# A two-layer decoder trunk on one core: the first layer's GpSimd steps named for VectorE, a third PSUM bank for its output projection, sixteen turning transfers recorded over other pairs

## The chip, the cores and the metric

One core of one Trainium2 chip. The time is the device time of one execution in microseconds (us); the median of three runs is compared. TensorE (PE in the profile) multiplies, ScalarE (ACT), VectorE (DVE) and GpSimd (POOL) do the elementwise work, SyncE (SP) only issues DMAs. GpSimd issues some DMAs too.

## The reference

Input x is 1024 tokens by 1024 features, float32. Layer 0 is gated linear attention with 4 heads (key width 128, value width 256), layer 1 is dilated sliding-window attention with 8 query heads in 3 groups over one shared K/V. Cut to the part that the change touches:

```python
# layer 0
q, k, v, g, a_lr = split(x @ w_in)
log_a = log_sigmoid(a_lr @ w_a2 + b_a2) / 16          # per head and key channel
b = cumsum(log_a)                                      # within a chunk
o_t = q_t S_t,  S_t = diag(exp(log_a_t)) S_{t-1} + k_t^T v_t
o = o * rsqrt(mean(o * o) + 1e-5) * norm_g
x1 = layer_norm(alpha * x + (o * silu(g)) @ w_out)
# layer 1
k_sh, v_sh = rope(x1 @ w_k), x1 @ w_v
out = layer_norm(alpha * x1 + (windowed_attention(rope(x1 @ w_q), k_sh, v_sh) * silu(x1 @ w_g)) @ w_out2)
```

## The kernel before, in words

Matrices are kept in a float32 form that TensorE multiplies in three passes: each operand is split in a high part (`split_hi`, always on ACT) and a low part (`split_lo`, the difference, recorded as `S.vp`), and a product is high*high, high*low, low*high. That holds for weights (`wf` loaded, `wh` and `wl` split from it) and for activations.

The program is recorded step by step with an object `S` and then ordered by a planner (`Sched.order`). The planner gives every step a cost, keeps a clock for each engine, and again and again takes the step that can start first; among steps that could start at the same time it takes the one recorded earlier (`prio`, which `S.later(n)` moves by n). A step recorded as `S.vector` goes to DVE, one recorded as `S.vp` to DVE or POOL, whichever the planner can start first (if DVE could start as early and is cheaper, DVE). The planner lets no two steps of DVE and POOL that read SBUF in the same way overlap (`shares_port`). The result is a fixed order of instructions for each engine; on the chip each engine runs its own list in that order and waits on semaphores. All instructions are issued from one line of the planner (L469), so the profile's groups are told apart by tile names, not by lines.

The stages, in order of time:

1. A first projection gives the values of head 0 and the gate's low-rank rows (tiles `pro`), while x is split in `xh` and `xl`.
2. From quarters of x, four sums (`xg`, line 1077 on) feed seven-product block multiplications (`pairs`, tiles `sev`), which give q and k of all heads; between them `gate(h)` computes b per head (tiles `sp`, `mn`), and `ahead(3)` computes the seven level factors of head 3 (tiles `Xa`) ahead of time.
3. Per head: `levels(h)` makes for each of seven levels L the factor X = exp of differences of b, times q and k (`steps`, four elementwise steps of 128x512 and one exponential), multiplies blocks of X (tiles `lv`) and merges them in `AT`. `state_prep(h)` makes `qe` and `ke`. `chunks(h, g)` runs four chunks of 128 tokens: products with `AT` and with the state `S` into the two banks `po`, then the next state `S` (DVE, from bank `ms`); afterwards it squares, sums (`sq`), and scales the result, and `finish` multiplies by the gate and, for head 3, splits the result in `ogh` and `ogl`. Projections of the values and gates (`vac`, `acc`) are recorded between these and fill TensorE.
4. `out_ln(0, ...)`, once for each half of the tokens: the output projection in eight column blocks `et`, each a group of 24 matmuls in one PSUM bank, then the layer norm. `bank(layer, et)` names the bank; there are two of each of `acc`, `lv`, `po` and `ms`.
5. Layer 1: V, then K and a part of Q in 14 pairs of seven-product multiplications with `rope` after each; in the same stage `turn_x` turns x1 for the last step, in 16 pieces, each a chain of transfers through one buffer (`swx`): a transposing DMA into `xa`, a store `x1p`, a load `xb`, an ACT copy `xc`, a store `x1t`. Then scores and attention per head, and the last projection, which reads `x1t`.

The names that the change touches: `gate` (the step `mn - sp`), `steps` (two of its four elementwise steps, called for 21 levels by `levels` and for 7 by `ahead`), the four `xg` differences per quarter, `state_prep` (two steps of `ke`), `chunks` (the sum of the two squares), `bank`, and the loop over the pairs at the end of stage 5.

Of the kernel before, what the change touches and what calls it, by code (L numbers as in the profile page):

```python
# [7 lines left out]
F32 = mybir.dt.float32  # L8
# [617 lines left out]
def trunk(tc, xT, xp, wP, wA, wA12, wAv3, w2, wO, wK, wV0, wV12, wB, wOB, par_d,  # L626
          ident_d, lmask_d, cos_d, sin_d, bmask_d, rmask_d, tri_d, lnr_d, out):
    S = Sched(tc, lat=LAT, pad=PAD)
# [5 lines left out]
    ps = S.pool("ps", space="PSUM")  # L634
# [20 lines left out]
    def hs(half):  # L655
        return slice(half * 512, half * 512 + 512)
# [80 lines left out]
    def blk(x, j):  # L737
        return x[:, j * 128:j * 128 + 128]
# [145 lines left out]
    def layer_a(t2, t1, after):  # L884
# [6 lines left out]
        def front(name, kind, dt=F32):  # L891
            return t0.tile([128, 512], dt, name=name, tag=kind, bufs={"a": NA0, "d": 4}[kind])

        def whole(dt, name):
            return t0.tile([128, T], dt, name=name, tag="X", bufs=4)
# [15 lines left out]
        def keep(name, k, t):  # L911
            hi, lo = quarter(name, k)
            split_hi(hi, t)
            split_lo(lo, t, hi)
# [104 lines left out]
        def gate(h):  # L1019
            b = whole(F32, "b")  # L1020
            made["b", h] = dram.tile([128, T], F32, name=f"mb{h}")
            for half in range(2):
                r = hs(half)
                z = ps.tile([128, 512], F32, name="z", tag="ms", bufs=2)
                S.tensor.matmul(z, w2t[:, h * 128:h * 128 + 128], aT[:, r], start=True, stop=True)
                sp = front("sp", "a")
                S.scalar.activation(sp, z, AF.Abs, bias=b2c[:, h:h + 1])
                S.scalar.activation(sp, sp, AF.Exp, scale=-1.0)
                S.scalar.activation(sp, sp, AF.Ln, bias=onec)
                mn = front("mn", "a")  # L1030
                S.vector.tensor_scalar(mn, z, b2c[:, h:h + 1], 0.0, op0=OP.add, op1=OP.min)
                S.vp.tensor_sub(mn, mn, sp)
                for c0 in (0, 256):
                    S.vector.tensor_tensor_scan(b[:, half * 512 + c0:half * 512 + c0 + 256], smask,
                                                 mn[:, c0:c0 + 256], 0.0, op0=OP.mult, op1=OP.add)
            S.sync.dma_start(made["b", h], b)

        def steps(b, q, k, L, X):
            n = T // (2 * L)
            view = lambda t: t.rearrange("p (n s l) -> p n s l", s=2, l=L)  # L1040
            bv, Xv = view(b), view(X)
            ref = bv[:, :, 0, L - 1:L].to_broadcast([128, n, L])
            S.vector.tensor_sub(Xv[:, :, 1, :], bv[:, :, 1, :], ref)
            S.vp.tensor_sub(Xv[:, :, 0, :], ref, bv[:, :, 0, :])
            S.scalar.activation(X, X, AF.Exp, scale=1.0 / 16.0)
            S.vector.tensor_mul(Xv[:, :, 1, :], Xv[:, :, 1, :], view(q)[:, :, 1, :])
            S.vp.tensor_mul(Xv[:, :, 0, :], Xv[:, :, 0, :], view(k)[:, :, 0, :])

        def ahead(h):
            q, k = spare(F32, "qa"), spare(F32, "ka")  # L1050
# [18 lines left out]
        with S.later(-500):  # L1069
            for k in range(4):  # L1070
                two = []
                for ct in (k, k + 4):
                    x = whole(F32, "xg")
                    S.sync.dma_start(x, xT[ct * 128:ct * 128 + 128])
                    two.append((x[:, hs(0)], x[:, hs(1)]))
                (old, t), (old2, low) = two
                S.vp.tensor_sub(old, t, old)
                S.vp.tensor_sub(t, low, t)
                keep("T3", k, t)
                keep("T1", k, old)  # L1080
                S.vp.tensor_sub(low, low, old)
                S.vp.tensor_sub(old2, old2, low)
                keep("T4", k, old2)
                keep("T2", k, low)

# [156 lines left out]
        def state_prep(h):  # L1242
            q, k, b = H[h]["q"], H[h]["k"], H[h]["b"]
            bc = b.rearrange("p (n c) -> p n c", c=128)
            qe = t2.tile([128, T], F32, name="qe", bufs=1)
            S.scalar.activation(qe, b, AF.Exp, scale=1.0 / 16.0)
            dec = t2.tile([128, NCH], F32, name="dec", bufs=2)
            S.vector.tensor_copy(dec, qe.rearrange("p (n c) -> p n c", c=128)[:, :, 127])
            S.vector.tensor_mul(qe, qe, q)
            ke = xtile(F32, "ke")  # L1250
            S.vp.tensor_sub(ke.rearrange("p (n c) -> p n c", c=128),
                                 bc[:, :, 127:128].to_broadcast([128, NCH, 128]), bc)
            S.scalar.activation(ke, ke, AF.Exp, scale=1.0 / 16.0)
            S.vp.tensor_mul(ke, ke, k)
            kh = t2.tile([128, T], F32, name="kh", bufs=2)
            for g in range(2):
                turn_blocks(kh[:, g * 512:g * 512 + 512],
                            [blk(ke, c) for c in range(4 * g, 4 * g + 4)])
            H[h].update(qe=qe, dec=dec, kh=kh, S=None)

        def chunks(h, g):
            v, qe, dec, kh = (H[h][n] for n in ("v", "qe", "dec", "kh"))
            AT = ATs[h % 2]
            oT = t2.tile([128, 2, 512], F32, name="oT", bufs=2)
            H[h]["oT", g] = oT
            St = H[h]["S"]
            po = [ps.tile([128, 512], F32, name="lv" if h == GH - 1 and g else "po", bufs=2) for _ in range(2)]
            for c in range(4):
                cc = 4 * g + c
                cs = slice(c * 128, c * 128 + 128)  # L1270
                for e in range(2):
                    es = slice(e * 128, e * 128 + 128)
                    out = po[e][:, cs].rearrange("p (s x r) -> p x s r", s=2, x=16)
                    S.tensor.matmul(out, v[g][:, c, es], natural(AT[:, cc, :]), start=True, stop=(cc == 0))
                    if cc:
                        S.tensor.matmul(out, St[:, es], natural(blk(qe, cc)), start=False, stop=True)
                if cc < NCH - 1:
                    pS = ps.tile([128, 256], F32, name="ms", bufs=2)
                    S.tensor.matmul(pS, blk(kh, cc), v[g][:, c, :], start=True, stop=True)
                    Sn = t2.tile([128, 256], F32, name="S", bufs=2)  # L1280
                    with S.later(-EVAC):
                        if cc:
                            S.vector.scalar_tensor_tensor(Sn, St, dec[:, cc:cc + 1], pS, op0=OP.mult, op1=OP.add)
                        else:
                            S.vector.tensor_copy(Sn, pS)
                    St = Sn
            H[h]["S"] = St
            sq = [t2.tile([128, 512], F32, name="sq", bufs=3) for _ in range(2)]
            for e in range(2):
                S.scalar.activation(sq[e], po[e], AF.Square)  # L1290
                S.va.copy(oT[:, e, :], po[e])
            S.vp.tensor_add(sq[0], sq[0], sq[1])
            sh, sl = (t2.tile([128, 512], FR, name="sq", bufs=3) for _ in range(2))
            split_hi(sh, sq[0])
            split_lo(sl, sq[0], sh)
            ss = ps.tile([128, 512], F32, name="ms", bufs=2)
            with S.group():
                S.tensor.matmul(ss, onesr, sh, start=True, stop=False)
                S.tensor.matmul(ss, onesr, sl, start=False, stop=True)
            R = t2.tile([128, 512], F32, name="sq", bufs=3)  # L1300
            rsqrt_rows(R, ss, 1.0 / 256.0, sq[0], epsq)
            for e in range(2):
                S.vector.tensor_mul(oT[:, e, :], oT[:, e, :], R)
# [44 lines left out]
            split_lo(lo[:, hs(half)], f, hi[:, hs(half)])  # L1348

    def bank(layer, et):  # L1350
        return ps.tile([128, 512], F32, name=("acc", "lv", "po")[et % 3 if layer else 0], bufs=2)

    def out_ln(layer, r, w_of, res, emit):
        n = r.stop - r.start
# [124 lines left out]
    def layer_b(xs, early):  # L1479
# [102 lines left out]
        for n, (a, b, g) in enumerate(jobs):  # L1582
            now = w
            if n + 1 < len(jobs):
                w = load_pair([x[0] for x in jobs[n + 1][:2]])
            pgs = [spare(F32, "pair") for _ in range(2)]
            seven(now, lambda i, hf, acc: rope(pgs[i], g, hf, acc))
            for x, pg in zip((a, b), pgs):
                S.sync.dma_start(x[1], pg)
            if n in [1, 2, 3, 4, 5, 6, 7, 8]:  # L1590
                with S.later(300):
                    for i in range(2):
                        turn_x(*divmod([1, 2, 3, 4, 5, 6, 7, 8].index(n) * 2 + i, 4))

        def reload_k(c):
            for g in (2, 1, 0):
# [446 lines left out]
```

## Time and profile before

| what | value |
|---|---|
| median of 3 runs | 1114.76 us (1113.89 to 1115.56) |
| the profiled execution | 1115.34 us, of which the span from the first to the last instruction is 1113.6 us |
| TensorE busy | 1096.0 us (98%), 7532 matmuls |
| DVE busy | 879.6 us (79%), 1735 instructions |
| ACT busy | 651.9 us (59%), 1329 instructions |
| POOL busy | 297.4 us (27%), 299 instructions |
| mean granted TensorE clock | 0.995 of full speed |

How to read it: TensorE is busy nearly all the time, so any time that can be gained on the other engines shows only where TensorE stood still for them. Matmuls overlap one another, so a group's mean duration is longer than the distance between two. In a row of a group, "x5 | 10.6, 2134" means five instructions, 10.6 us in all, 2134 ns each, and behind the second bar stands the time that the engine was idle just before them, with what ended it.

### The profile page before, as it was taken

The page shows a single profiled execution, that of the slowest core. Times are in us where ns is not written, and L with a number is a line of the kernel's source. Part 1 is how long each engine was busy: PE and PEld are TensorE (multiplying, and loading weights), DVE is VectorE, ACT ScalarE, POOL GpSimd, SP SyncE. Part 2 cuts the span into 40 slices and gives each one's busy share as a digit, 9 for nine tenths or more (in the row PEclk, how much of TensorE's full clock was granted, in tenths as well). Part 3 has the DMA queues.
Part 4 walks back from the last instruction along what each step waited for, and adds up shares of the span by engine and source line. Part 5 has one row for each costly group of instructions (what it writes and reads, how often), then busy time and mean ns, then how long its engine had stood idle before and what let it go on. Part 6 is the DMA issues. An engine that isn't in the chain of part 4 may idle for free.

```text
span 1113.6 us, 20296 instructions
## 1 busy us (share of the span) xinstructions
PE 1096.0 (98%) x7532; PEld 934.5 (84%) x7532; DVE 879.6 (79%) x1735; ACT 651.9 (59%) x1329; POOL 297.4 (27%) x299
## 2 busy tenths in 40 slices
PE   9999999999999999999999999999999999999997
PEld 9988888887887888888878888888888888888886
DVE  5886979998568589887878888986678778896588
ACT  5565535665555256656566666665677787673252
POOL 0322200232012022012444344332233454340010
PEclk9999999999999999999999999999999999999999
DMA  8467773144352446757766776769633552342544
GB/s 291 147 210 207 242 289 117 59 152 135 116 189 92 155 136 215 208 175 164 168 173 185 183 192 179 170 185 269 184 96 121 173 167 94 113 140 76 184 147 171
DMA packets 92627, 185.71 MB, mean 167 GB/s; under 512 B 16912, under 2 KB 38032, under 8 KB 92528
## 3 DMA queue, kind: packets, MB, share of 16 engines
q1 hardware_dynamic: 84320, 167.11, 45.8%
q0 software_dynamic: 8208, 17.31, 9.2%
q8 instruction: 59, 0.97, 0.3%
q14 instruction: 40, 0.33, 0.1%
HBM read 134.57 MB, written 47.71 MB: 164 GB/s over the span
## 4 chain that ended last, share of the span: by engine, by line
PE 91%; DVE 4%; ACT 2%; DMA 1%; issue 1%; POOL 0%; DVEq 0%; ACTq 0%; POOLq 0%
PE acc L469 31%; PE sev L469 27%; PE po L469 10%; PE lv L469 9%; PE vac L469 8%; PE ms L469 3%; PE pro L469 3%; DMA wf<-in_wB 1%; DVE X L469 1%; DMA wf<-in_wK 1%; DVE sum L469 1%; DVE wl L469 1%; DVE rt L469 0%; ACT wh L469 0%; ACT t L469 0%
## 5 line engine op out<-in xcount | busy, mean ns | idle before, releaser
L469 ACT ACTIVATE wh<-wf 128x1024 fp32r<-128x1024 f32 (+3 forms) x118 | 99.4, 844 | 96.5 <-PE acc L469 47.7
L469 PE MATMUL sev<-T,wh 128*128 128x512 f32 x448 | 137.8, 389 | 0.0
L469 PEld LDWEIGHTS sev<-T,wh 128*128 128x128 f32 x448 | 84.1, 188 | 17.4
L469 PE MATMUL sev<-T,wl 128*128 128x512 f32 x224 | 87.1, 389 | 0.0
L469 PE MATMUL lv<-K,Q 128*64 128x64 f32 (+2 forms) x512 | 71.4, 287 | 0.4 <-DVE sts L469 0.4
L469 PE MATMUL acc<-x1h,wh 128*128 128x512 f32 x160 | 71.0, 444 | 0.0
L469 DVE TENSOR_TENSOR wl<-wf,wh 128x1024 fp32r<-128x1024 f32 (+3 forms) x55 | 61.6, 1124 | 9.2 <-ACT wh L469 9.0
L469 PE MATMUL acc<-x1h,wl 128*128 128x512 f32 x160 | 62.8, 392 | 0.0
L469 PE MATMUL acc<-x1l,wh 128*128 128x512 f32 x160 | 62.6, 391 | 0.0
L469 PE MATMUL acc<-ogh,wh 128*128 128x512 f32 x152 | 60.1, 395 | 0.5 <-ACT ogh L469 0.4
L469 PE MATMUL acc<-ogl,wh 128*128 128x512 f32 x152 | 59.4, 391 | 0.9 <-DVE ogl L469 0.9
L469 PE MATMUL acc<-ogh,wl 128*128 128x512 f32 x152 | 59.2, 390 | 0.0
L469 PEld LDWEIGHTS lv<-K,Q 128*64 128x64 f32 (+1 forms) x512 | 51.5, 164 | 8.9 <-DVE sts L469 1.3
L469 DVE CUSTOM_DVE_ANT_0 P<-lv,bmask 128x256 f32<-128x256 f32 (+1 forms) x128 | 47.1, 378 | 14.9 <-PE lv L469 11.3
L469 POOL DMA_DIRECT2D wl<-in_wB x42 | 37.1, 890 | 81.2 <-ACT wl L469 79.0
L469 ACT ACTIVATE P<-P,sts 128x64 f32<-128x64 f32 (+2 forms) x128 | 49.9, 392 | 13.4 <-DVE sts L469 13.1
L469 POOL TENSOR_TENSOR pair<-t,t 128x512 f32<-128x512 f32 x26 | 43.5, 1674 | 41.7 <-DVE t L469 31.0
L469 DVE TENSOR_TENSOR u<-u,sev 128x512 f32<-128x512 f32 x54 | 36.6, 682 | 21.2 <-PE sev L469 20.7
L469 PE MATMUL acc<-xh,wh 128*128 128x512 f32 x128 | 53.1, 415 | 0.0
L469 ACT ACTIVATE t<-u 64x512 f32<-64x512 f32 x56 | 35.4, 631 | 28.9 <-DVE u L469 18.1
L469 PE MATMUL acc<-xh,wl 128*128 128x512 f32 x128 | 50.3, 393 | 0.0
L469 PE MATMUL acc<-xl,wh 128*128 128x512 f32 x128 | 50.2, 392 | 0.0
(354 smaller groups left out, 3394.8 us busy)
## 6 DMA issues: line engine op xcount, KB each, us to landing
wf<-in_wB SPq DMA_DIRECT2D x32, 512.0 KB, 7.4
wf<-in_wA SPq DMA_DIRECT2D x24, 512.0 KB, 4.3
qd<-pair SPq DMA_DIRECT2D x22, 512.0 KB, 4.8
Q<-qd SPq DMA_DIRECT2D x22, 512.0 KB, 7.0
wl<-in_wB POOLq DMA_DIRECT2D x33, 256.0 KB, 7.8
wf<-in_wO SPq DMA_DIRECT2D x16, 512.0 KB, 3.6
wf<-in_wOB SPq DMA_DIRECT2D x16, 512.0 KB, 3.5
wf<-in_wV SPq DMA_DIRECT2D x10, 512.0 KB, 3.9
```

What stands on the lines that cost most here:

```text
L469: getattr(handle[o.eng], meth)(*[conv(a) for a in args], **{k: conv(v) for k, v in kw.items()})
```

## The change

Three edits.

First, nine calls in layer 0 that were recorded as `S.vp` (DVE or POOL) are recorded as `S.vector` (DVE alone): in `gate`, `steps`, the `xg` sums, `state_prep` and `chunks`. Other steps of layer 0 stay with `S.vp`: every `split_lo`, the sums of weights and products in `pairs`, the clearing of `aT`, `AT` and `Dg`, and in `out_ln` the sums `lnA` and `a2`.

Second, `bank(0, et)` was always `acc` (two banks); it becomes `acc`, `acc`, `po` in turn.

Third, the recording of the 16 `turn_x` pieces: before, two after each of the pairs 1 to 8; after, piece i after pair 2 + 10 i // 16, that is one or two after each of the pairs 2 to 11.

```diff
@@ gate
-                S.vp.tensor_sub(mn, mn, sp)
+                S.vector.tensor_sub(mn, mn, sp)
@@ steps
-            S.vp.tensor_sub(Xv[:, :, 0, :], ref, bv[:, :, 0, :])
+            S.vector.tensor_sub(Xv[:, :, 0, :], ref, bv[:, :, 0, :])
...
-            S.vp.tensor_mul(Xv[:, :, 0, :], Xv[:, :, 0, :], view(k)[:, :, 0, :])
+            S.vector.tensor_mul(Xv[:, :, 0, :], Xv[:, :, 0, :], view(k)[:, :, 0, :])
@@ the four differences of x, per quarter
-                S.vp.tensor_sub(old, t, old)
-                S.vp.tensor_sub(t, low, t)
+                S.vector.tensor_sub(old, t, old)
+                S.vector.tensor_sub(t, low, t)
...
-                S.vp.tensor_sub(low, low, old)
-                S.vp.tensor_sub(old2, old2, low)
+                S.vector.tensor_sub(low, low, old)
+                S.vector.tensor_sub(old2, old2, low)
@@ state_prep
-            S.vp.tensor_sub(ke.rearrange("p (n c) -> p n c", c=128),
+            S.vector.tensor_sub(ke.rearrange("p (n c) -> p n c", c=128),
                                  bc[:, :, 127:128].to_broadcast([128, NCH, 128]), bc)
...
-            S.vp.tensor_mul(ke, ke, k)
+            S.vector.tensor_mul(ke, ke, k)
@@ chunks
-            S.vp.tensor_add(sq[0], sq[0], sq[1])
+            S.vector.tensor_add(sq[0], sq[0], sq[1])
@@ bank
-        return ps.tile([128, 512], F32, name=("acc", "lv", "po")[et % 3 if layer else 0], bufs=2)
+        return ps.tile([128, 512], F32, name=("acc", "lv", "po")[et % 3] if layer else ("acc", "acc", "po")[et % 3], bufs=2)
@@ the pairs of layer 1
-            if n in [1, 2, 3, 4, 5, 6, 7, 8]:
-                with S.later(300):
-                    for i in range(2):
-                        turn_x(*divmod([1, 2, 3, 4, 5, 6, 7, 8].index(n) * 2 + i, 4))
+            with S.later(300):
+                for i in range(16):
+                    if 2 + i * 10 // 16 == n:
+                        turn_x(*divmod(i, 4))
```

## The prediction

> **What bounds the kernel now.** I read the busy shares first, then TensorE's own waits, then the clock in short windows, then around each wait the chain of waits and the instructions in order of time.
>
> The busy shares, and the waits of TensorE ("waited for: us in total, times, longest"):
>
> ```profile
> PE 1096.0 (98%) x7532; PEld 934.5 (84%) x7532; DVE 879.6 (79%) x1735; ACT 651.9 (59%) x1329; POOL 297.4 (27%) x299
> PE sev L469 <- ACT u L469: 3.0, 2, 2.6
> PE po L469 <- DVE S L469: 2.7, 2, 2.4
> PE lv L469 <- issue: 0.9, 1, 0.9
> PE acc L469 <- DVE ogl L469: 0.9, 1, 0.9
> PE acc L469 <- ACT ogh L469: 0.4, 1, 0.4
> ```
>
> TensorE is the bound. No edit takes a matmul away, so all that can be won is time in which TensorE stands still or runs slowly, and these rows are nearly all of that ahead of the end of the program. Two stops are long, and the windows show what follows each (columns: busy of PE, PEld, DVE, ACT, POOL, then the granted clock, DMA share, GB/s):
>
> ```profile
> 173.00:263.00 90.00, 88.65 (x1499) 74.44 (x1493) 84.83 (x134) 56.76 (x83) 23.61 (x13) 1.00 0.35 119
> 266.20:269.60 3.40, 3.40 (x13) 3.03 (x12) 2.41 (x4) 0.00 (x0) 0.00 (x0) 0.50 0.03 8
> 566.60:570.00 3.40, 3.08 (x7) 2.49 (x8) 3.40 (x6) 2.04 (x4) 1.19 (x1) 0.50 0.84 166
> ```
>
> Right behind the stop of 2.4 us (262 to 265) and behind that of 2.6 us (564 to 567) the granted clock is 0.50 for 3.4 us; half of 3.4 is 1.7 us lost on top of each. The first row is the stage in which heads 0 and 1 make their levels: DVE is busy 84.83 of 90 us there, so DVE is nearly full while POOL is busy 23.61.
>
> Why the first long stop: the chain of waits, then DVE and POOL in order of time (start, duration):
>
> ```profile
> 259.97 4.58 DVE X L469 x2
> 264.54 0.40 DVE S L469
> 259.86 2.79 DVE L469 TENSOR_TENSOR X<-X,k 128x512 f32<-128x512 f32 x1
> 262.57 1.97 DVE L469 TENSOR_TENSOR X<-X,q 128x512 f32<-128x512 f32 x1
> 259.70 2.40 POOL L469 TENSOR_TENSOR ke<-ke,k 128x1024 f32<-128x1024 f32 x1 [7.51 <-ACT ke L469]
> 262.06 1.94 POOL L469 TENSOR_TENSOR X<-X,k 128x512 f32<-128x512 f32 x1
> L469 DVE TENSOR_TENSOR X<-X,k x16: 678/684/2794, 167.0 to 259.9; 128x512 f32<-128x512 f32 x16
> L469 DVE TENSOR_TENSOR ke<-ke,k x3: 1214/1217/1227, 190.0 to 299.9; 128x1024 f32<-128x1024 f32 x3
> ```
>
> A DVE product of 128x512 takes 0.68 us (median); these two took 2.79 and 1.97, and each ended 0.5 us after POOL's instruction beside it. DVE stood still while POOL worked, and the next state S, for which TensorE waited, stood behind.
>
> **The change part by part.** *Moving the arithmetic.* What POOL did of it in the whole first layer, and the one group that stays with it:
>
> ```profile
> L469 POOL TENSOR_TENSOR X<-X,k 128x512 f32<-128x512 f32 x5 | 10.6, 2134 | 17.8 <-ACT X L469 17.8
> L469 POOL TENSOR_TENSOR xg<-xg 128x512 f32<-128x512 f32 x4 | 7.8, 1955 | 17.0 <-DMA xg<-in_xT 9.0 <-DVE xg L469 8.0
> L469 POOL TENSOR_TENSOR X<-b 128x512 f32<-128x512 f32 x4 | 6.2, 1540 | 28.7 <-DVE wl L469 27.7 <-PE lv L469 1.0
> L469 POOL TENSOR_TENSOR sq<-sq 128x512 f32<-128x512 f32 x4 | 5.2, 1291 | 40.4 <-ACT sq L469 40.4
> L469 POOL TENSOR_TENSOR Xa<-Xa,ka 128x512 f32<-128x512 f32 x2 | 3.5, 1756 | 10.3 <-ACT Xa L469 10.3
> L469 POOL TENSOR_TENSOR wl<-wf,wh 128x1024 fp32r<-128x1024 f32 x3 | 7.1, 2373 | 63.1 <-PE ms L469 46.0 <-ACT wh L469 17.1
> ```
>
> With two of `ke` and one of `mn` that is 22 instructions. In the full stage 173 to 263 fall all of X, one sum of squares and both `ke`:
>
> ```profile
> L469 POOL TENSOR_TENSOR sq<-sq 128x512 f32<-128x512 f32 x1 | 1.3, 1301 | 8.7 <-ACT sq L469 8.7
> L469 POOL TENSOR_TENSOR ke<-b 128x1024 f32<-128x1024 f32 x1 | 1.9, 1897 | 0.7 <-PE lv L469 0.7
> ```
>  DVE pays there 10 x 0.68 + 2 x 1.22 = 9.3 us more. What it gets back is the time that it stood still; means against the medians 0.68 (128x512) and 1.22 (128x1024):
>
> ```profile
> L469 DVE TENSOR_TENSOR X<-b 128x512 f32<-128x512 f32 x29 | 21.2, 760 | 0.7 <-PE lv L469 0.7
> L469 DVE TENSOR_TENSOR X<-X,q 128x512 f32<-128x512 f32 x18 | 15.1, 853 | 0.0
> L469 DVE TENSOR_TENSOR X<-X,k 128x512 f32<-128x512 f32 x13 | 11.3, 885 | 0.0
> L469 DVE TENSOR_TENSOR sq<-sq 128x512 fp32r<-128x512 f32 (+1 forms) x5 | 4.4, 883 | 0.0
> L469 DVE TENSOR_TENSOR qe<-qe,q 128x1024 f32<-128x1024 f32 x2 | 3.2, 1622 | 0.1
> ```
>
> 29 x 0.08 + 18 x 0.17 + 13 x 0.20 + 5 x 0.20 + 2 x 0.40 = 9.8 us. So DVE's load in the full stage stays where it is (+9.3 - 9.8), but each moved step ends in 0.7 or 1.2 us instead of 1.5 to 2.4. At the first stop: the two stretched products give back 2.79 + 1.97 - 2 x 0.68 = 3.4 us, POOL's two steps cost DVE 1.22 + 0.68 = 1.9, S comes 1.5 us earlier, and the stop of 2.4 falls to 0.9. A stop of 0.9 ("lv, issue") has no window of half clock behind it, those of 2.4 and 2.6 have, so I count the 1.7 as gone too: 3.2 us. Bounds: 0 (another order with the same stop) and 2.4 + 1.7 = 4.1. The other 0.3 of the row "po from DVE S" I count as gone, 0 to 0.3.
>
> The rows of POOL show a wait for ACT (17.8 at X, 40.4 at sq), which now stands in DVE's queue, with S, the copies of `po` and the splits behind it. DVE's own X<-X,k and sq instructions above waited 0.0, because DVE has other steps to do until ACT is done: price 0, bounded above by 17.8 / 5 = 3.6 us for one that is placed badly. Outside the full stage the moved xg, Xa, mn and sq cost DVE 10 x 0.68 = 7 us, hidden under TensorE, which waits in no row there for DVE but at `ogl`. The moved steps issue no DMAs. POOL's own accumulating loads of weights get a freer queue; that is worth nothing, since they wait for ACT's copies.
>
> [...]
>
> *The third bank.* TensorE stops at 347 and 348 for the last head's `ogh` and `ogl`:
>
> ```profile
> 346.65 1.27 POOL L469 TENSOR_TENSOR sq<-sq 128x512 f32<-128x512 f32 x1 [3.92 <-ACT sq L469]
> 347.21 1.86 DVE L469 TENSOR_TENSOR ogl<-oT,ogh 128x512 fp32r<-128x512 f32 x2
> 348.52 0.19 PEld L469 LDWEIGHTS acc<-ogl,wh 128*128 128x128 f32 x1 [1.20 <-DVE ogl L469]
> ```
>
> With two banks the column blocks 0 and 1 are begun, and a third can't be until one is done. A third bank gives TensorE 18 matmuls of block 2 (six kt that need no last head) to do meanwhile, and POOL's `sq` leaves DVE free. Both edits aim at the same stop, 0.4 + 0.9 = 1.3 us in the waits; I take it once, bounds 0 and 1.3. A loss is excluded: bank `po` is next wanted by layer 1's V, two column blocks (10 us) after block 5 leaves it. In the rest of the output projection no wait for a bank is in TensorE's rows, so nothing else is to be had there.
>
> *The turning transfers.* When they run now (times are first and last start), and the next user of their buffer:
>
> ```profile
> L469 ACT ACTIVATE xc<-xb x16: 767/780/797, 484.9 to 744.0; 128x512 uint16<-128x512 uint16 x16
> L469 SPq DMA_TRANSPOSE xa<-x1d x16: 1193/1316/2190, 461.5 to 725.9; - x16
> L469 SPq DMA_DIRECT2D xb<-x1p x16: 319/358/482, 475.5 to 738.2; - x16
> L469 DVE TENSOR_TENSOR swx<-sts,par x6: 285/286/2319, 796.5 to 966.8; 128x128 f32<-128x128 f32 x4, 128x64 f32<-128x64 f32 x2
> ```
>
> (744.0 - 484.9) / 15 = 17.3 us from one to the next: they already run one at a time from before the first pair to the 13th, because each waits for the one buffer and the planner starts what can start, whatever pair recorded it. The edit moves only their rank in ties on ACT (0.78 each) and SP. I count 0. If the whole chain slipped by a pair (some 19 us), the last `xc` would be at 763, ahead of 796.5 where the buffer is wanted. Bounds: the stop at 564, 2.6 + 1.7 = 4.3 us, gone, or one more like it.
>
> That stop has another cause, in steps that aren't touched:
>
> ```profile
> 560.24 1.29 POOL t L469
> 561.53 1.71 POOL pair L469
> 566.27 0.61 ACT u L469
> ```
>
> This is the rope of layer 1, still DVE's or POOL's: POOL's slow sums hold ACT, and ACT holds TensorE. A new order may keep it, lose it or bring another; one such stop in 14 pairs is what this order has, so one is what I expect of the next.
>
> **The sum.** 3.2 + 0.3 + 1.3 + 0 = 4.8 us. The profiled execution took 1115.34 us (span 1113.6), 0.58 above the median; 1115.34 - 4.8 - 0.58 = 1110.0.
>
> **The rivals.**
>
> *DVE becomes the bound (slower).* In the stage 173 to 263 DVE has 90 - 84.83 = 5.2 us left and gets 9.3 us of work. If it gets back what it lost (9.8), nothing changes; but POOL still has the splits, 2.4 us for a `wl` of 128x1024 (three of them before), and the planner may give it more of these now that it is free, each of which holds DVE as the X steps did. It decides when less than 9.3 - 5.2 = 4.1 us of the 9.8 come back: then DVE, not TensorE, ends the stage. With nothing back, TensorE stands still 4.1 us longer with 1.7 of half clock behind it, and the other gains are buried: 1114.8 + 5.8 = 1120.6. For it speaks that DVE has hardly a gap there now; against it, that the planner knows that the two can't overlap and put just one `wl` on POOL in that stage while X was free to go there.
>
> [...]
>
> *The stops only move (no change).* The order of every engine's list is made anew, and the stop at 262 is the outcome of one order. If S is again late once by over 2 us, the 3.2 doesn't come, and with 1.3 or 0.3 left the time is 1113.2 to 1114.8, say 1114.5. For it: TensorE's other S waits came to 0.3 us in all, so the stop of 2.4 is a single accident that a new order can repeat. Against it: its cause, two POOL steps of 2.4 and 1.9 us in a row, can't recur with these steps.
>
> *Also layer 1's stop goes (faster still).* The new order or the other ranks of `xc` on ACT take away the stop of 2.6 us and its half clock: 1110.0 - 4.3 = 1105.7. For it: an `xc` of 0.78 us stands in ACT's list in that stage. Against it: its rope steps and sums are as before.
>
> *The third edit does nothing* is part of my forecast. If it did spread the transfers, and they were in the way, it would look like the case above.
>
> **How the numbers follow.** The runs shown differ by 1.67 us, so 0.2% (2.2 us) is about what can be told from no change: faster is below 1112.5, slower above 1117.0. The forecast, 1110.0 with its own range of 1107 to 1112.4, has 0.46; layer 1's stop gone as well, 1105.7, has 0.13; moved stops, 1114.5, have 0.19; DVE as the bound, 1120.6 at its full price and about 1118 at half of it, has 0.22. So faster 0.59, same 0.19, slower 0.22. The fastest bound is every wait of the list gone: 1110.0 less 0.9 (rest of the S stop), 0.9 (lv) and 3.0 + 1.7 (layer 1) = 1103.5. The range goes from there to 1118.5, inside the slower case, of which about half is left out.
>
> **What the profile after will show.** Right: no POOL row of X, Xa, ke, xg, mn or of the sum of squares ahead of the output projection; DVE's X rows with means near 0.69; in 173 to 263 DVE's busy time near 85 again; no window of half clock around 266; `acc` and `po` as banks of the output projection, and its wait at 347 gone; `xc` still one every 17 to 18 us from before the first pair. Wrong: POOL's `wl` rows ahead of the output projection up from three, with DVE rows still stretched beside them; a wait of `po` or `lv` for DVE longer than 2 us; a second or third window at 0.50; `xc` gathered elsewhere, with weights (`wf`) later on the SP queue. The prediction is wrong above all if the new order brings one stop with half clock more than it takes away, which is worth 4 us either way.

## The result, and the profile after

The median is 1107.89 us (4 runs, 1107.55 to 1108.76) against 1115.16 (4 runs, 1113.89 to 1116.62): a ratio of 0.9942, interval 0.9926 to 0.9958, or 7.3 us. In a second group of runs the ratio was 0.9935 (0.9922 to 0.9948). The profiled execution took 1108.76 us, its span is 1107.0 against 1113.6. In the groups of runs below, three executions that took 1214, 3055 and 6280 us (two of the kernel before, one of the second edit alone) are left out of the ratios.

The page, TensorE's waits, and windows of the kernel after (columns as before):

```profile
PE 1093.0 (99%) x7532; PEld 933.5 (84%) x7532; DVE 878.1 (79%) x1756; ACT 651.3 (59%) x1326; POOL 263.1 (24%) x281
PE sev L469 <- ACT u L469: 2.2, 1, 2.2
PE lv L469 <- issue: 1.4, 2, 1.1
PE vac L469 <- issue: 0.7, 1, 0.7
PE acc L469 <- POOL wol L469: 0.4, 1, 0.4
173.00:263.00 90.00, 89.00 (x1479) 75.47 (x1467) 85.58 (x150) 55.94 (x79) 0.00 (x0) 1.00 0.34 119
559.40:562.70 3.30, 3.30 (x9) 2.52 (x9) 3.30 (x5) 1.44 (x3) 1.28 (x1) 0.50 0.83 123
```

The rows "po from DVE S", "acc from DVE ogl" and "acc from ACT ogh" are gone; the wait for u in layer 1 is still there, with its window of half clock. In the full stage 173 to 263 POOL does nothing any more, and DVE is busy 85.58 us where it was 84.83. DVE's groups there, and the rows of POOL ahead of the output projection:

```profile
L469 DVE TENSOR_TENSOR X<-b 128x512 f32<-128x512 f32 x33 | 21.6, 686 | 0.0
L469 DVE TENSOR_TENSOR X<-X,k 128x512 f32<-128x512 f32 x18 | 12.3, 685 | 0.0
L469 DVE TENSOR_TENSOR X<-X,q 128x512 f32<-128x512 f32 x17 | 11.6, 685 | 0.0
L469 POOL TENSOR_TENSOR wl<-wf,wh 128x1024 fp32r<-128x1024 f32 x3 | 7.1, 2377 | 194.4 <-PE ms L469 191.0 <-ACT wh L469 3.4
L469 POOL TENSOR_TENSOR tT<-xg,tT 128x512 fp32r<-128x512 f32 x5 | 6.6, 1323 | 30.4 <-ACT tT L469 30.4
```

Means of 760, 885 and 853 ns have become 686, 685 and 685: more instructions in the same busy time, because none is stretched. What the third bank does is in the chain of waits (start, us, what):

```profile
340.87 1.37 PE acc L469 x6
342.24 2.72 PE po L469 x12
344.96 2.73 PE acc L469 x12
```

Where TensorE had stopped for `ogh` and `ogl`, it runs twelve matmuls of column block 2 in `po` for 2.72 us and goes on without a wait.

Where the 6.6 us of span came from, by the starts of the same matmuls in both traces:

| up to | start before | start after | gained since the row above |
|---|---|---|---|
| first product `vac` | 132.72 | 132.33 | 0.39 |
| first product with `ogh` | 333.38 | 328.84 | 4.15 |
| first product with `x1h` | 429.26 | 422.48 | 2.24 |
| last of the pairs in layer 1 | 768.40 | 760.81 | 0.81 |
| end of the span | 1113.57 | 1106.99 | -1.01 |

The last row is a loss. Of it 0.7 us lie at the start of the last projection, where TensorE now waits for `wol`, the low part of its weights (the last row of waits above); the kernel before has no such wait.

### The profile page after: what moved, and what is told of

The parts are those of the page before. It is cut to its first block, busy times and chain, and to the rows that moved or that the text cites. A ratio compares the mean times of both kernels' runs of the same rounds, so it can differ in the third digit from the quotient of the medians.

```text
span 1107.0 us, 20264 instructions
## 1 busy us (share of the span) xinstructions
PE 1093.0 (99%) x7532; PEld 933.5 (84%) x7532; DVE 878.1 (79%) x1756; ACT 651.3 (59%) x1326; POOL 263.1 (24%) x281
## 4 chain that ended last, share of the span: by engine, by line
PE 94%; DVE 2%; DMA 2%; ACT 1%; issue 1%; POOL 0%; DVEq 0%; ACTq 0%; POOLq 0%
PE acc L469 30%; PE sev L469 28%; PE po L469 11%; PE lv L469 9%; PE vac L469 8%; PE ms L469 4%; PE pro L469 3%; DMA wf<-in_wOB 1%; DMA wf<-in_wB 1%; DVE wl L469 0%; ACT wl L469 0%; DVE rt L469 0%; ACT t L469 0%; ACT wh L469 0%; DVE wol L469 0%
## 5 line engine op out<-in xcount | busy, mean ns | idle before, releaser
L469 POOL TENSOR_TENSOR wl<-wf,wh 128x1024 fp32r<-128x1024 f32 x6 | 14.3, 2386 | 228.4 <-PE ms L469 192.4
L469 PEld LDWEIGHTS sev<-T,wl 128*128 128x128 f32 x224 | 42.0, 188 | 8.7
L469 PE MATMUL acc<-ogh,wh 128*128 128x512 f32 x120 | 47.4, 395 | 0.0
```

The source lines that it names most:

```text
L469: getattr(handle[o.eng], meth)(*[conv(a) for a in args], **{k: conv(v) for k, v in kw.items()})
```

## The experiments

Each ratio is against the kernel before, run in the same group.

**The first edit alone** (two banks and the old pairs otherwise).

> Only the first edit: the ten calls of the first layer on VectorE, two banks and the old pairs. Theory (VectorE stood still beside GpSimd, and the state S with it): the stop of 2.4 us near 262 and the half clock behind it go, which is 2.4 + 1.7 = 4.1 us, so about 1111 us; the stop near 347 stays in part (0.4 to 1.3 us). Rival (the third bank or the other ranks of the transfers carry the gain): less than 2 us below the kernel before, above 1113 us.

1109.7 us, 0.9958 (0.9945 to 0.9972): 4.7 us. The first product with `ogh` starts at 328.12, 5.3 us earlier than before. The wait for S is gone, a wait for `ogl` stays, now on POOL:

```profile
PE acc L469 <- POOL ogl L469: 0.8, 1, 0.8
PE acc L469 <- ACT ogh L469: 0.4, 1, 0.4
```

**The second edit alone.**

> Only the second edit: acc, acc, po in turn for the first layer's output projection, GpSimd's arithmetic as before. Theory: the wait for ogh and ogl near 347 (1.3 us) and a short one near 417 (0.3 us) go, and nothing else: 1 to 2 us below the kernel before, about 1113.5 us, with the half clock at 266 still there. Rival (a third bank loosens the whole order): 3 us or more.

1111.14 us, 0.9966 (0.9953 to 0.9979): 3.8 us, more than the 1.3 of the prediction and the 1 to 2 of the theory. Its profile keeps the wait for S and the half clock behind it:

```profile
PE po L469 <- DVE S L469: 2.7, 2, 2.4
265.90:269.30 3.40, 3.40 (x14) 3.02 (x13) 2.41 (x4) 0.00 (x0) 0.00 (x0) 0.50 0.18 11
```

The waits for `ogh` and `ogl` are gone. Up to the first `ogh` nothing is gained (333.51 against 333.38), and the first product with `x1h` starts at 427.15, 2.1 us earlier than before: that is as far as the mechanism goes, and the rival's whole order loosened is not seen, though its figure of 3 us came true. Another 1.3 us come in the pairs of layer 1, whose last product starts at 765.02 against 768.40. The stop for u there is at most 2.0 us, and no window of half clock follows it; the granted clock of that stage is 1.00 where it was 0.99:

```profile
PE sev L469 <- ACT u L469: 3.1, 3, 2.0
480.00:770.00 290.00, 286.95 (x1308) 238.59 (x1307) 239.38 (x323) 182.31 (x316) 113.93 (x94) 1.00 0.71 182
```

At the start of the last projection 1.7 us of the lead are lost again, where TensorE waits for `wol` (0.8 and 0.3 us). Whether this execution is like the kernel's others isn't shown: it took 1113.62, 2.5 us above their median.

**The third edit alone.**

> Only the third edit: the turning pieces recorded after pairs 2 to 11. Theory (they run one at a time through one buffer, whatever pair records them): xc still every 17 to 18 us from before the first pair on, time within 0.5 us of the kernel before, 1115 us. Rival (spreading them clears the stop of the first pair, 0.6 us, or that of the third, 2.6 + 1.7 us): 0.6 or 4.3 us faster.

1114.44 us, 0.9995 (0.9984 to 1.0006): nothing. The transfers run as they did:

```profile
L469 ACT ACTIVATE xc<-xb x16: 772/788/807, 484.1 to 744.3; 128x512 uint16<-128x512 uint16 x16
```

**The order before, the engine changed.** The planner plans as before and its order is kept; only the engine that runs the first edit's calls (ten in the diff, not nine) is set afterwards:

```diff
         done = self.order()
+        for o in done:
+            if id(o) in self.to_dve:   # the calls of the first edit
+                o.eng = "DVE"
```

> The kernel before, planned with the same costs and in the same order, but the 22 instructions of the ten calls that the plan gives to GpSimd are put in VectorE's list at their planned place. [...] Rival (the gain is the new order, in which S stands ahead of the products): VectorE's list is only longer, the stop stays at 2 us or more with its half clock, 1115 us or above.

1110.07 us, 0.9961 (0.9946 to 0.9977), as the first edit with its new order. DVE's rows in 173 to 263:

```profile
L474 DVE TENSOR_TENSOR X<-b 128x512 f32<-128x512 f32 x33 | 21.9, 692 | 0.7 <-PE lv L474 0.7
L474 DVE TENSOR_TENSOR X<-X,q 128x512 f32<-128x512 f32 x18 | 12.1, 684 | 0.0
```

With the same order of steps the stretching is gone and TensorE has no wait for S left. For the first edit it is the engine that carries the gain, not the new order.

**The order after, the engine set back.** In the changed kernel, the same way, the 21 products X * k and the four products ke * k are put on POOL.

> The changed kernel in its own order, but the 21 products X * k of heads 0 to 2 and the four products ke * k are issued on GpSimd instead of VectorE. Theory (the engine, not the order, made the stops): each product takes 1.3 to 2.9 us and holds VectorE, stops of TensorE for S or X of 1 to 3 us come back and half clocks with them: 1112 to 1118 us. Rival (the order of the changed kernel carries the gain): 1108 us.

1114.52 us, 0.9999 (0.9990 to 1.0008): the whole gain is gone.

```profile
L473 DVE TENSOR_TENSOR X<-b 128x512 f32<-128x512 f32 x33 | 26.4, 837 | 0.0
L473 POOL TENSOR_TENSOR X<-X,k 128x512 f32<-128x512 f32 x17 | 32.5, 1922 | 46.1 <-ACT X L473 37.3 <-PE acc L473 8.8
PE ms L473 <- POOL ke L473: 2.4, 1, 2.4
PE po L473 <- DVE S L473: 2.0, 3, 1.0
```

X * k takes 1.92 us on POOL, and DVE's X<-b beside it 0.84 instead of 0.69. Here two costs are mixed: DVE held up (S, 2.0) and TensorE waiting for POOL's own slow product (ke, 2.4). This layer loses more than the first edit gave: the first `ogh` starts at 334.60, 5.8 us later than in the changed kernel. The third bank's gain is kept (93.64 us from there to the first `x1h`, as in the changed kernel; 95.88 before). The other 3.2 us are lost in layer 1, which this edit doesn't touch: its stop for u is 3.4 us long here, with half clock for 6.7.

**GpSimd work for which nobody waits.** To tell these two apart:

```diff
+                if id(o) in self.beside:   # the products X * k of heads 0 to 2
+                    dst, x = self.beside[id(o)]   # dst: the tile aS, not read again
...
+                    for c in (0, 256, 512, 768):
+                        nc.gpsimd.tensor_add(dst, x[:, c:c + 128].make(), x[:, c + 128:c + 256].make())
```

> The changed kernel in its own order, and after each of the 21 products X * k of the first layer GpSimd adds four pairs of 128 columns of that X into a tile that nobody reads again (some 1.6 us each time, 34 us in all). Nobody waits for these sums but the reuse of X five levels later. [...] Rival (only the slowness of GpSimd's own steps cost time): as the changed kernel, 1108 us.

1116.72 us, 1.0021 (1.0011 to 1.0031), 10 us above the changed kernel in the same group (1106.32).

```profile
L470 DVE TENSOR_TENSOR X<-b 128x512 f32<-128x512 f32 x31 | 23.5, 785 | 0.9 <-POOL aS L475 0.9
L475 POOL TENSOR_TENSOR aS<-X x84: 453/792/7097, 167.1 to 275.4; 128x128 f32<-128x128 f32 x84
PE po L470 <- DVE S L470: 4.1, 3, 3.3
```

Sums that serve nothing bring the stop for S back, longer than before (3.3 us), and half clock behind it (0.50 from 214.6 to 217.9). The first `ogh` starts at 339.80, 11.0 us later than in the changed kernel, so the loss lies in this layer. DVE's own wait for these sums, at the reuse of X, is a small part: 2.5 us in two waits, 0.9 of them in the first row. Both sides are longer here: DVE's X<-b has a mean of 785 ns where the changed kernel has 686, and POOL's sum of 128 columns takes 0.45 us at its shortest and 0.79 at the median.

**The first two edits, the transfers as before.**

> The first and the second edit with the turning pieces recorded as before. Theory (the third edit does nothing, the other two add): as the changed kernel, 1106 to 1108 us. Rival (the third edit matters once the other stops are gone): 1110 us.

1105.79 us, 0.9924 (0.9912 to 0.9936): the third edit adds nothing here either. In this execution the stop for u is shorter than in the changed kernel (2.2 us there), and the mean granted clock over the span is 0.999 (0.996 there):

```profile
PE sev L469 <- ACT u L469: 1.1, 1, 1.1
```

**More of the same.** Four kernels go on from the changed one. First the first layer's `split_lo` on `S.vector` too:

> The changed kernel, and the first layer's splits (low parts of weights and activations up to the output projection) on VectorE too, so that GpSimd reads SBUF there only for the sums of the pairs. Theory: what is left of stretched VectorE time ahead of the output projection is 4.4 us in the stage of the four differences and 2.4 us from 280 to 350, where TensorE doesn't wait for it: within 1 us of the changed kernel, 1106 to 1108 us. Rival (any GpSimd step in the first layer costs): 1104 us.

1110.82 us, 0.9967 (0.9955 to 0.9979): slower than the changed kernel, which neither the theory nor the rival expected.

```profile
PE vac L469 <- issue: 2.9, 1, 2.9
```

Its first `vac` product is already 1.6 us late (133.92 against 132.33), and then comes a stop of 2.9 us at 176 that the changed kernel has as 0.7. These two are the whole loss: the first `ogh` is 3.7 us late (332.52 against 328.84). The profile names no releaser for the stop, so what it waits for stays open.

The rope's two steps on `S.vector`, and then its last sum alone:

> The changed kernel, and the two steps of the rope in layer 1 (t2 * sin and the sum into pair) on VectorE too, 40 instructions that GpSimd had in part. Theory: as in the first layer, VectorE gives back what it stood still beside GpSimd (28 us in the stage of the pairs) and pays some 30 us, and the stop of 2.2 us in the third pair goes, with its half clock where that follows: 2 to 4 us below the changed kernel, near 1105 us. Rival (VectorE becomes the bound, 220 of 269 us in the stage before): more waits of TensorE for u and t, 1109 us or more.

> The changed kernel, and of the rope the last sum alone (into pair) on VectorE, 26 instructions of GpSimd's. Theory: the stop in the third pair, where a copy of ACT waits for GpSimd's sum into pair, falls under 1 us: 1104.5 to 1106.5 us. Rival (the weights set that stop, and GpSimd's sum only stands beside it): 1106.5 to 1108 us.

1105.63 us, 0.9927 (0.9912 to 0.9941), and 1105.97 us, 0.9923 (0.9910 to 0.9936). Both lie within the intervals of the changed kernel: no slower, not shown to be faster. The wait for u in their profiles:

```profile
PE sev L469 <- ACT u L469: 1.5, 1, 1.5
PE sev L469 <- ACT u L469: 1.5, 2, 1.1
```

Shorter than 2.2, but neither gone nor, for the second, under the 1 us that was expected. Neither has half clock behind it (the granted clock from 501 to 763 is 1.00 in both); but the kernel of the first two edits has a stop of 1.1 us without half clock too (mean 0.999), with the rope as it was, so the rope's engine isn't shown to be the reason. With the rope, the sums of products and of weights in the pairs as well:

> The changed kernel, and both the rope and the sums of products and of weights in the pairs on VectorE, so that GpSimd keeps just the splits and its DMAs there. Theory (VectorE stops standing still, as in the first layer): the stop of 2 us in the third pair goes, 1104 to 1106 us. Rival (the two thirds of GpSimd's work that go were help in this stage, VectorE has 46 of 262 us left in it): 1109 us or more.

1113.27 us, 0.9994 (0.9983 to 1.0004): the rival was right, though at other places than it said.

```profile
PE lv L469 <- DVE sts L469: 2.7, 2, 1.6
PE sev L469 <- ACT u L469: 2.3, 1, 2.3
83.20:86.60 3.40, 3.40 (x9) 2.63 (x9) 1.61 (x3) 1.58 (x4) 0.90 (x1) 0.50 0.97 364
```

The pairs' code serves both layers, and the stop of 2.3 us with its half clock is now in the first layer's pairs, at 79, ahead of the levels. In layer 1 the theory holds: the stop for u in the third pair is gone. Behind the pairs the kernel loses again, in the waits for `sts` above.

The changed kernel once more stood in the second group:

> The changed kernel once more, beside the others of this group. Theory: the first edit gives some 4.5 us and the second 2 to 4, the third nothing, so 6.5 to 8 us below the kernel before, near 1108 us. Rival (the two edits remove parts of the same stops and don't add): 4 to 5 us below, near 1110.5 us.

1106.32 us, 0.9935, that is 7.2 us. Alone the first edit gave 0.42%, the second 0.34%, the third 0.05%; together 0.65%, and the first two 0.76%. They add, within the intervals. None of the other versions is shown to beat the changed kernel.

## Why the prediction was right

It said 4.8 us from 1114.76; 7.3 were measured. The direction and the mechanism held, two terms of the sum were too small, and a part of the difference is luck with half clocks (last section).

- *DVE's load stays, its steps end earlier.* Right: 85.58 against 84.83 us of 90, and no X row stretched. The kept order with the engine changed shows that this carries the edit.
- *The stop for S, 3.2 us.* Under-sized: the prediction let 0.9 us of the stop stand, and it went whole, with its half clock: 4.15 us up to the first `ogh`, the 0.3 included, against 3.5 counted. The step that failed is the charge of 1.9 us for POOL's two steps, put ahead of S. The first row is the kernel before, the others the order before with the engine changed:

```profile
264.46 1.05 DVE L469 SCALAR_TENSOR_TENSOR S<-S,dec,ms 128x256 f32<-128x256 f32 x2
259.98 0.69 DVE L474 TENSOR_TENSOR X<-X,k 128x512 f32<-128x512 f32 x1
261.19 0.48 DVE L474 SCALAR_TENSOR_TENSOR S<-S,dec,ms 128x256 f32<-128x256 f32 x1
261.58 1.22 DVE L474 TENSOR_TENSOR ke<-ke,k 128x1024 f32<-128x1024 f32 x1
264.53 0.69 DVE L474 TENSOR_TENSOR X<-X,k 128x512 f32<-128x512 f32 x1
```

The first of the two products starts as late as before (259.98 against 259.86), so DVE was not late until then. The two moved steps run behind S (261.58 and 264.53). S therefore gets nearly the whole 3.4 us that the two products give back: it starts 3.3 us earlier, not 1.5. In the changed kernel it starts at 261.38.

- *The third bank, 1.3 us, with the same stop for both edits.* Under-sized and the coupling wrong: 2.24 us between `ogh` and `x1h`, in the second edit alone as in the changed kernel. The waits' 1.3 us counted the idle time between modelled ends; three matmuls there start at 346.39, 347.14 and 348.52 where others are 0.23 apart, which is 1.7 us. Another 0.3 lie at 418.25, where a matmul starts 0.52 behind the one before it; the prediction saw nothing to be had there. The first edit alone left the stop in place (0.8 + 0.4), on another engine.
- *The transfers, 0.* Right, shown by the third edit alone and by leaving it out. The transfers kept their times; that the chain through one buffer is what keeps them there is argued, not tested.
- *Layer 1: "a new order may keep it, lose it or bring another".* Right, and all three were seen: the changed kernel keeps a stop of 2.2 us with half clock, the first two edits have one of 1.1 without, the products set back on GpSimd have one of 3.4 with twice the half clock. The attention's `swx` steps start at 788.8 where they had started at 796.5: in the changed kernel layer 1 ran the same work 7.7 us earlier, with the stop still in the third pair.

```profile
L469 DVE TENSOR_TENSOR swx<-sts,par x6: 284/288/2281, 788.8 to 959.2; 128x128 f32<-128x128 f32 x4, 128x64 f32<-128x64 f32 x2
```

- *The slower rival.* Its condition, that POOL takes more splits, came true only in part: `tT` went from two to five, all ahead of the full stage, and `wl` stayed at three, all behind it. That its mechanism is real the 84 idle sums show, which cost 10 us.
- *DVE beside POOL.* From 173 to 263 DVE's X steps have means of 0.69 us where POOL does nothing beside them (after), of 0.76 to 0.89 beside 23.6 us of POOL's work (before), of 0.84 and 0.95 beside 37.9 us (the products set back on GpSimd) and of 0.76 to 0.79 beside 62.6 us (the idle sums).

## What to carry to other kernels

Work on a second engine isn't free just because that engine is idle: here, by the prediction's estimates, DVE lost 9.8 us beside POOL in the full stage, and the moved work cost it 9.3. Look at the mean duration of the first engine's groups against their median, and if what they lose is as much as the moved work would cost, move it back. Do that where the waits show who is late; the same edit on other steps lost half of the gain (the splits) or all of it (the sums of the pairs). And ask where the moved step will stand in the list: only what stands ahead of the awaited step is charged to it (here the two moved steps ran behind S, at 261.58 and 264.53, and S came 3.3 us earlier, not 1.5). And look at when a step runs now before changing where it is recorded.

## What was not expected of the hardware

In these runs a stop's length does not by itself decide on the half clock. These windows stand behind a stop of 2.9 us (the first layer's splits on DVE), of 1.9 us (the changed kernel, second profile) and of 3.4 us (the products set back on GpSimd):

```profile
179.40:182.80 3.40, 3.40 (x15) 2.82 (x16) 1.55 (x4) 0.66 (x2) 0.00 (x0) 1.00 0.00 0
559.80:563.20 3.40, 3.40 (x9) 2.62 (x9) 3.40 (x5) 1.47 (x3) 1.27 (x1) 0.51 0.82 120
565.20:571.90 6.70, 5.86 (x14) 4.62 (x15) 4.56 (x7) 2.81 (x6) 1.57 (x2) 0.50 0.86 217
```

Full clock behind 2.9 us, half behind 1.9 for 3.4 us, half behind 3.4 for twice as long (6.7). So the 1.7 us that the prediction hung on each stop is a chance, not a price.

The clock records in the traces show one regularity. Each such window lasts 3.413 us in the kernel before and in the changed kernel, and the stretches at full clock ahead of a window and between two are whole multiples of that: 259.413 and 296.960 us in the kernel before (76 and 87 times), 552.959 us in the changed kernel (162 times). Beside the idle sums the windows stand at 214.6 to 217.9 and 303.3 to 306.6, 85.4 us apart (25 times). What decides whether half clock follows a stop, these runs don't show.

How many windows an execution gets differs. In the profiled executions shown above the mean granted clock over the span goes with their number ahead of the last matmul: two of 3.4 us (the kernel before, the idle sums) or one of twice that (the products set back on GpSimd) at 0.995, one at 0.996 (the changed kernel in both profiles, the sums of the pairs on DVE) or 0.997 (the second edit alone). A window costs 1.7 of some 1107 us, 0.0015 of the mean, so 0.998 and 0.999 are taken as none. By this mark, which is an estimate, 64 of 73 executions of the kernel before had at least one, and 3 of 10 of the changed kernel. The executions without any have medians of 1112.7 and 1106.7 us, 6.0 apart; by the same estimate some 1.3 of the 7.3 us come from such windows, where the prediction counted 1.7 for the one at 266 alone.
